# A two-layer hybrid trunk on one core: moving the second layer's set-up beside the first layer's gate and up products, and making the second layer's first product in passes

## The chip, the core and the metric

One core of a Trainium2 chip runs the whole program, in one launch. The metric is the device time from the first to the last instruction, with what the runtime adds around it, in microseconds (us). Each of the core's engines works through its own queue in order: TensorE (PE; its weight loads are PEld), VectorE (DVE), ScalarE (ACT), GpSimd (POOL) and SyncE (SP), which here only issues DMA transfers. Engines wait for each other and for transfers on semaphores.

## The reference

The program is a decoder trunk of two layers over 1024 tokens of width 1024, in float32. Each layer normalises its input, projects it once to 1440 columns, and gives these to three mixers: sliding-window attention, a state-space layer, and latent attention. The outputs are joined, projected back and added; then a normalised SwiGLU feed-forward part follows. What the change touches is the parameter arithmetic of the state-space layer and the order of the work around it:

```python
for l in range(DEPTH):
    h = rms_norm(x, ln1_g[l])
    proj = h @ w_in[l]
    q_a, k_a, v_a, u_b, c_q, c_kv, k_r = jnp.split(proj, IN_SPLITS, axis=-1)
    o_a = swa_attention(q_a, k_a, v_a, sinks[l], bias)
    o_b = s5_mixer(u_b, ssm_a_re[l], ssm_a_im[l], ssm_log_dt[l], ...)
    o_c = mla_attention(c_q, c_kv, k_r, positions, ...)
    x = x + jnp.concatenate([o_a, o_b, o_c], axis=-1) @ w_out[l]
    h = rms_norm(x, ln2_g[l])
    x = x + (jax.nn.silu(h @ w_gate[l]) * (h @ w_up[l])) @ w_down[l]
return rms_norm(x, final_g)

# in s5_mixer, per layer, from the parameters alone:
lam = lax.complex(a_re, a_im); dt = jnp.exp(log_dt)
a_bar = jnp.exp(lam * dt[:, None])                    # 16 groups x 64 states
b_bar = ((a_bar - 1.0) / lam)[..., None] * bmat
```

## The kernel before, in words

**Precision.** A float32 operand is split into a high part (a rounded copy, made by ScalarE) and a low part (the rest, made by VectorE or GpSimd). A product takes three matmuls: high by high, high by low, low by high (`mm3s`, `product`).

**Set-up.** `setup` runs once at the start, before the first layer. It loads x and transposes it, and then, at a lower priority, calls `setup_ssm` for both layers at once: the parameters of two layers lie side by side in 16 columns, 8 for each layer, and the angles and magnitudes of the powers of `a_bar` are made on VectorE in tiles of 128x640 (`ph`) and 128x256 (`e1`), with two sines on ScalarE. A loop over q (two for each layer) then writes one row of parameters each, `sp`, to the DRAM tensor `spd`. `ssm_tables(l, f)` (f is 0 or 1) reads such a row back as `par`, and makes from it the tables of one half of a layer's state-space part: complex products on VectorE (`cmul`, L966) and, for the last one, on GpSimd; transposes (L998, L1022) and small matmuls (L1036, L1037) on TensorE in the one bank `s5`; copies on ScalarE; and writes to the DRAM tensors `tabd` and `lagd`. The first layer's two calls stand in `setup`, followed by the rotary set-up (`setup_rope`). The second layer's two calls stand in the first layer's feed-forward part, after pair 2 and after pair 6 of its gate and up products.

**Feed-forward.** Gate and up, and down, are Strassen-like: an operand is cut in 2x2 blocks, and seven products replace eight. In `ffn`, `ffn_begin` makes the first products of pairs 0 to 3 ahead, and `ffn_pair` then makes the others, 14 products of 12 matmuls for a full pair, for eleven pairs; it yields after each product, before the product's bank is evacuated. Down runs over windows of (column block d, first pair, end pair), `WINDOWS`. At the first window of a d the residual x tiles 2d and 2d+1 are loaded from `xe`; the last window has d = 2 and is worked in the order `LAST` = (1, 6, 2, 7, 4, 5, 3). While gate and up run, the x tiles 2 to 7 are free; the tables use them as scratch (`Lent`).

**Change of layers.** The blocks of the feed-forward operand are tiles b{block}{slot}, with slots 3, 0, 1, 2, of which pool 1 holds 16. `normed` puts the next layer's normalised input, high and low part for each k and half h, into these tiles in the order of `BLOCKS[1]`, k in the order `KORD` = (0, 1, 6, 7, 2, 3, 4, 5). So a part can be written when the last down window has made its last product with the block. Then `in_u` and `project_plain` make the first product of the next layer: 24 matmuls for half 0, 24 for half 1, and behind them (`scales`) the sums of squares and the scale factors.

**Order of work.** The program is traced in the order of the Python code. A scheduler then simulates it, and puts each engine's queue in order by priority (place in the trace) and simulated readiness, so instructions can move ahead of their place. `issue_after(ins)` adds, for instructions traced in its block on the engine of `ins`, that they stand behind `ins` in that engine's queue; it adds no semaphore.

The lines that the prediction names: L231, L237, L240 and L243 are the helpers `tt`, `ts`, `stt` and `act`; L247 and L248 the high and low part of a split; L271 to L273 the three matmuls of `mm3s`; L534 the write to `spd`, L979 its read; L1001 the copies of C out of the bank; L1635 the feed-forward matmuls; L1892 the load of the residual.

## Time and profile before

| | us |
|---|---|
| median of three runs (2316.06 to 2323.11) | 2319.89 |
| profiled execution, its own time | 2313.62 |
| its span, first to last instruction | 2311.8 |
| TensorE matmuls in flight | 2172.3 |
| VectorE busy | 1637.8 |
| GpSimd busy | 1171.5 |
| ScalarE busy | 990.9 |

The profiled execution is one run of the program; it need not be one of the three that are timed. Busy times count an engine's instructions in flight. Matmuls overlap, so TensorE's row is not its share of peak, and its gaps are more telling than its sum. In the lists, an instruction's row gives start, time, engine, line, operation, output and input tiles (buffer numbers left out), shapes and count, and in brackets the idle time before it with what released it. [...]

### The profile page before, as it was taken

How to read it: one execution, taken by the hardware profiler on the slowest of the kernel's cores; microseconds unless marked ns; L12 is line 12 of the kernel's file. 1: busy time of each engine (PE TensorE's matmuls, PEld its weight loads, DVE VectorE, ACT ScalarE, POOL GpSimd, SP SyncE). 2: the span in 40 equal slices, each digit the busy share in tenths (PEclk: the TensorE clock that was granted, in tenths of full speed). 3: DMA queues.
4: the chain of work that ended last, by engine and by line, in shares of the span. 5: the costliest groups of instructions: out<-in, count | busy, mean ns of one | idle time of the engine just before them, and what ended most of it. 6: DMA issues, size and time to landing. Idle time of an engine off the chain costs nothing. (4 is left out here: it accounts for less than half of the span.)

```text
span 2311.8 us, 31478 instructions
## 1 busy us (share of the span) xinstructions
PE 2172.3 (94%) x10414; PEld 1775.8 (77%) x10414; DVE 1637.8 (71%) x2909; ACT 990.9 (43%) x1981; POOL 1171.5 (51%) x1038
## 2 busy tenths in 40 slices
PE   7699879999899999999979998799999999999998
PEld 6488768887778878788768886687877888877886
DVE  6677975559777677876855578655777756688767
ACT  5254665544232333444433456544522333254444
POOL 1263653134465555677743354530445555567765
PEclk9799999999999999999989999899999999999999
DMA  7622334543443353753333232535454332355422
GB/s 258 177 76 72 108 102 147 177 121 105 164 136 114 108 167 101 227 151 105 114 105 89 63 106 64 158 104 177 142 163 145 101 110 96 110 173 179 141 89 80
DMA packets 288300, 296.26 MB, mean 128 GB/s; under 512 B 43665, under 2 KB 213512, under 8 KB 288008
## 3 DMA queue, kind: packets, MB, share of 16 engines
q1 hardware_dynamic: 288136, 294.23, 41.6%
q8 instruction: 83, 1.36, 0.2%
q14 instruction: 81, 0.66, 0.1%
HBM read 204.63 MB, written 83.23 MB: 125 GB/s over the span
## 5 line engine op out<-in xcount | busy, mean ns | idle before, releaser
L1635 PE MATMUL f<-b,wt 128*128 128x512 f32 x3219 | 772.6, 395 | 20.0 <-ACT wt L247 5.1
L248 POOL TENSOR_TENSOR wt<-raw,wt 128x512 fp32r<-128x512 f32 (+3 forms) x332 | 497.9, 1506 | 534.7 <-ACT wt L247 398.1
L1635 PEld LDWEIGHTS f<-b,wt 128*128 128x128 f32 x3219 | 605.7, 189 | 164.3 <-ACT wt L247 7.1
L1635 PE MATMUL g<-b,wt 128*128 128x512 f32 x1965 | 477.9, 395 | 9.5 <-DVE gc L231 8.3
L1635 PEld LDWEIGHTS g<-b,wt 128*128 128x128 f32 x1965 | 370.0, 189 | 97.2 <-issue 10.5
L248 POOL TENSOR_TENSOR wt<-S,wt 128x512 fp32r<-128x512 f32 (+2 forms) x222 | 293.6, 1327 | 266.5 <-ACT wt L247 252.7
L247 ACT CAST wt<-raw 128x512 fp32r<-128x512 f32 (+3 forms) x356 | 229.3, 648 | 352.2 <-PE g L1635 93.9
L247 ACT CAST wt<-S 128x512 fp32r<-128x512 f32 (+2 forms) x222 | 126.2, 573 | 263.5 <-DVE S L1577 163.6
L271 PE MATMUL mm<-b,wt 128*128 128x512 f32 x320 | 131.4, 411 | 14.3 <-ACT b L243 13.5
L272 PE MATMUL mm<-b,wt 128*128 128x512 f32 x320 | 128.5, 402 | 0.9 <-DVE b L240 0.9
L273 PE MATMUL mm<-b,wt 128*128 128x512 f32 x320 | 128.2, 401 | 0.0
L248 DVE TENSOR_TENSOR tl<-pt,th 128x512 fp32r<-128x512 f32 (+2 forms) x176 | 96.4, 553 | 44.3 <-ACT th L247 41.9
L1577 DVE TENSOR_TENSOR S<-raw,raw 128x512 f32<-128x512 f32 (+2 forms) x74 | 65.5, 888 | 74.2 <-DMA raw<-in_w_gate 39.8
L247 ACT CAST th<-pt 128x512 fp32r<-128x512 f32 (+2 forms) x176 | 83.3, 477 | 78.9 <-PE pt L1308 41.4
L1290 POOL TENSOR_SCALAR pr<-pr,den 128x128 f32<-128x128 f32 (+3 forms) x64 | 49.1, 770 | 90.9 <-DVE den L1289 89.3
L1577 DVE TENSOR_TENSOR S<-raw,S 128x512 f32<-128x512 f32 (+2 forms) x74 | 81.9, 1110 | 13.2 <-POOL wt L248 13.1
L1635 PE MATMUL s<-b,wt 128*128 128x512 f32 x360 | 88.4, 393 | 2.2 <-DVE x L240 2.0
L902 POOL TENSOR_SCALAR pr<-pr,den 128x256 f32<-128x256 f32 (+1 forms) x128 | 70.6, 564 | 27.5 <-DVE den L900 22.1
L271 PEld LDWEIGHTS mm<-b,wt 128*128 128x128 f32 x320 | 62.0, 194 | 28.2 <-ACT b L243 14.6
L1635 PEld LDWEIGHTS s<-b,wt 128*128 128x128 f32 x360 | 67.8, 189 | 17.4 <-DVE x L240 2.5
L243 ACT ACTIVATE t<-B 128x512 f32<-128x512 f32 x44 | 27.8, 633 | 117.3 <-DVE B L231 116.6
L1281 PE MATMUL sc<-k,q 96*128 96x512 f32 (+7 forms) x288 | 73.0, 379 | 3.7 <-ACT pr L243 3.5
(472 smaller groups left out, 4124.0 us busy)
## 6 DMA issues: line engine op xcount, KB each, us to landing
raw<-in_w_gate SPq DMA_DIRECT2D x52, 512.0 KB, 4.0
raw<-in_w_up SPq DMA_DIRECT2D x52, 512.0 KB, 5.1
actd<-gc SPq DMA_DIRECT2D x102, 256.0 KB, 2.0
raw<-in_w_out SPq DMA_DIRECT2D x32, 512.0 KB, 3.9
B<-actd SPq DMA_DIRECT2D x62, 256.0 KB, 2.7
raw<-in_w_down SPq DMA_DIRECT2D x40, 384.0 KB, 3.3
x<-xe SPq DMA_DIRECT2D x48, 256.0 KB, 3.0
raw<-in_w_in SPq DMA_DIRECT2D x22, 512.0 KB, 5.3
```

Source lines behind the costliest of these rows:

```text
L243: self.A.activation(out=out, in_=a, func=func, **kw)
L247: self.A.copy(hi, src)
L248: (eng or self.V).tensor_tensor(out=lo, in0=src, in1=hi.bitcast(F32), op=ALU.subtract)
L271: self.T.matmul(ps, wh, xh, start=(i == 0), stop=False)
L272: self.T.matmul(ps, wh, xl, start=False, stop=False)
L273: self.T.matmul(ps, wl, xh, start=False, stop=(i == n - 1))
L902: self.G.tensor_scalar(out=pr[:, j, lo_k:256], in0=pr[:, j, lo_k:256], scalar1=den[:, j:j + 1], scalar2=0.0, op0=ALU.mult, op1=ALU.add)
L1281: self.T.matmul(o, q[a][rows, qs], k[kh][c][rows, 0:w], start=(x == 0), stop=(x == 2 and not last))
L1290: self.G.tensor_scalar(out=pr[:, 0:nk], in0=pr[:, 0:nk], scalar1=den[:, 0:1], scalar2=0.0, op0=ALU.mult, op1=ALU.add)
L1577: tt = lambda o, x, y, op: (self.G if b in self.gpre else self.V).tensor_tensor(out=o, in0=x, in1=y, op=op)
L1635: mm = lambda w, x, i: self.T.matmul(p, w, x, start=(i == 0 and not onto), stop=(i == 3 * n - 1), skip_group_check=onto)
```

## The change

1. `setup` calls `setup_ssm` for layer 0 alone, with 8 columns in place of 16. The 8 columns of layer 1's three parameters are kept in a small tile.
2. In the first layer's `ffn`, layer 1's `setup_ssm` and both calls of `ssm_tables` are recorded: their engine calls go to a list, not to the engines. After each product of pairs 4 to 10 three entries of the list are issued, on TensorE behind the last matmul and on VectorE behind the last `tt` or `stt`; what is left over is issued after the last pair. The set-up's tiles come from the same x tiles as the tables' (`Shelf`), and the row of parameters is one tile for each q.
3. The order of `BLOCKS[1]` is other: slot 3 of the five blocks first, as before, but then all slots of block 6, of 7, of 4, of 5, and of 3.
4. In the second layer `project_plain` makes its first product in passes over both halves: high weights by high input, low weights by high input, then high weights by low input, in turns of eight matmuls.
5. In `normed` for the second layer, the low parts of the last four k are placed on VectorE behind the last recorded `tt` or `stt`. `gained` itself is no longer recorded in `last_v`.

```diff
-BLOCKS = [[(b, k) for k in SLOTS for b in bs] for bs in ((1, 2), (6, 7, 4, 5, 3))]
+BLOCKS = [[(b, k) for k in SLOTS for b in (1, 2)], [(b, SLOTS[0]) for b in (6, 7, 4, 5, 3)]]
+BLOCKS[1] += [(b, k) for b in (6, 7, 4, 5, 3) for k in SLOTS[1:]]
 BLOCKS[1:] = BLOCKS[1][:16], BLOCKS[1][16:]
...
+class Recorder:
+    def __init__(self, engine, log):
+        self.engine, self.log = engine, log
+    def __getattr__(self, name):
+        return lambda *a, **k: self.log.append((getattr(self.engine, name), a, k))
...
-        self.V.tensor_tensor(out=out, in0=a, in1=b, op=op)
+        self.last_v = self.V.tensor_tensor(out=out, in0=a, in1=b, op=op) or self.last_v
...
         with self.tc.high_priority(offset=-LATE):
-            self.setup_ssm(st, cols, logdt, n16)
+            a_re, a_im = (cols[:, spans[x]:spans[x] + n16] for x in ("a_re", "a_im"))
+            self.ssm_in = [(a_re, a_im, logdt)]
+            for i in range(1, L):
+                keep = cp.tile([128, 3, 8], F32, f"ssm_in{i}")
+                for j, x in enumerate(self.ssm_in[0]):
+                    self.V.tensor_copy(keep[:, j], x[:, 8 * i:8 * i + 8])
+                self.ssm_in.append([keep[:, j] for j in range(3)])
+            self.setup_ssm(st, 0)
             self.setup_bias(st, ps)
...
-    def setup_ssm(self, st, cols, logdt, n):
-        are = cols[:, self.spans["a_re"]:self.spans["a_re"] + n]
-        aim = cols[:, self.spans["a_im"]:self.spans["a_im"] + n]
+    def setup_ssm(self, st, l):
+        n = 8
+        are, aim, logdt = (x[:, 0:n] for x in self.ssm_in[l])
...
-        sp = st.tile([128, 2 * self.depth, NSP], F32, "sp")
-        for q in range(2 * self.depth):
+        for q in range(2):
+            par = st.tile([128, NSP], F32, f"sp{q}")
...
-            self.dma(out=self.spd[q], in_=sp[:, q, :])
+            self.dma(out=self.spd[2 * l + q], in_=par)
...
     def project_plain(self, l, c0, evac, w=None, then=None, tag=("mm", 2)):
         wh, wl = w or self.in_weights(l, c0)
         done = []
+        if l and then is not None:
+            done = [self.mps.tile([128, 512], F32, *tag) for _ in range(2)]
+            passes = [(wh, 0, k) for k in KORD] + [(wl, 0, k) for k in KORD] + [(wh, 1, k) for k in KORD]
+            for a in range(0, 24, 8):
+                for h, p in enumerate(done):
+                    for i in range(a, a + 8):
+                        x, j, k = passes[i]
+                        self.T.matmul(p, x[:, k, :], self.h[h][k][j], start=(i == 0), stop=(i == 23))
+            then(2)
+            for h, p in enumerate(done):
+                evac(h, p)
+            return
...
-            self.gained(self.xT[k][h], self.spans["ln1"] + 8 * l + k, t[k])
+            order = self.tc.issue_after(self.last_v.ins) if l and n > 3 else contextlib.nullcontext()
+            with order:
+                self.gained(self.xT[k][h], self.spans["ln1"] + 8 * l + k, t[k])
...
+    def recorded(self, *parts):
+        for part in parts:
+            log = []
+            kept = self.V, self.A, self.T, self.G, self.dma
+            self.V, self.A, self.T, self.G = (Recorder(e, log) for e in kept[:4])
+            self.dma = lambda **k: log.append((kept[4], (), k))
+            part()
+            self.V, self.A, self.T, self.G, self.dma = kept
+            for f, a, k in log:
+                with self.tc.issue_after(self.last.ins), self.tc.issue_after(self.last_v.ins):
+                    f(*a, **k)
+                yield
...
         if more:
-            tabp = Lent([lambda i=i: self.x_tile(2 + i % 6, i // 6, False) for i in range(12)], ("bbr", "bbi", "cr", "ci", "dg"))
+            places = [lambda i=i: self.x_tile(2 + i % 6, i // 6, False) for i in range(12)]
+            tabp = Lent(places, ("bbr", "bbi", "cr", "ci", "dg"))
+            side = self.recorded(lambda: self.setup_ssm(Shelf(places), l + 1),
+                                 *(lambda f=f: self.ssm_tables(l + 1, f, tabp, ps, None) for f in range(2)))
         drain(ahead)
         for pair in range(FT // 2):
-            drain(self.ffn_pair(l, pair))
-            if more and pair in (2, 6):
-                with self.tc.issue_after(self.last.ins):
-                    self.ssm_tables(l + 1, pair // 4, tabp, ps, None)
+            for _ in self.ffn_pair(l, pair):
+                if more and pair > 3:
+                    next(side, None), next(side, None), next(side, None)
+        if more:
+            drain(side)
```

## Rows read from the trace of the kernel before

**Rows 1.** The page, part 1: busy us (share of span) x instructions.
```profile
PE 2172.3 (94%) x10414; PEld 1775.8 (77%) x10414; DVE 1637.8 (71%) x2909; ACT 990.9 (43%) x1981; POOL 1171.5 (51%) x1038
```

**Rows 2.** Windows at the start: length, busy PE, PEld, DVE, ACT, POOL, PEclk, DMA, GB/s.
```profile
65.00:84.40 19.40, 0.00 (x0) 0.00 (x0) 12.63 (x80) 2.30 (x3) 2.73 (x1) 0.58 0.61 154
84.40:92.00 7.60, 5.87 (x16) 3.81 (x17) 6.50 (x11) 2.40 (x5) 5.06 (x8) 0.51 0.58 172
```

**Rows 3.** Waits from 60 to 130 us: us in total, times, longest.
```profile
PE s L1022 <- DVE t L966: 19.6, 1, 19.6
...
DVE bbr L966 <- DMA par<-spd: 6.6, 1, 6.6
```

**Rows 4.** Timeline of VectorE at the start.
```profile
40.42 0.23 DVE L544 CAST rang<-pos 128x128 f32<-128x128 int32 x1 [2.22 <-DMA xd<-x]
...
67.74 0.20 DVE L510 COPY sp<-sn 128x96 f32<-128x96 f32 x1
...
74.07 0.47 DVE L231 TENSOR_TENSOR sp<-sp,q 128x4 f32<-128x4 f32 x4
```

**Rows 5.** Timeline of TensorE in the first layer's gate and up.
```profile
647.60 0.33 PE L998 MATMUL s<-ident,x 128*128 128x128 f32 x1 [4.72 <-DVE x L1001]
647.69 4.12 PE L1635 MATMUL g<-b,wt 128*128 128x512 f32 x10
```

**Rows 6.** Windows of 40 us in the first layer's gate and up.
```profile
740.00:780.00 40.00, 40.00 (x176) 32.73 (x175) 24.17 (x31) 12.56 (x21) 19.72 (x15) 1.00 0.32 101
780.00:820.00 40.00, 40.00 (x182) 32.20 (x181) 31.04 (x47) 12.69 (x23) 23.27 (x20) 1.00 0.37 117
```

**Rows 7.** Timeline of TensorE at the change of layers.
```profile
1186.98 0.76 PE L271 MATMUL mm<-b,wt 128*128 128x512 f32 x1 [12.27 <-ACT b L243]
```

**Rows 8.** Timeline of VectorE at the change of layers.
```profile
1175.84 2.83 DVE L240 SCALAR_TENSOR_TENSOR b<-x,gains,b 128x512 fp32r<-128x512 f32 x1
...
1186.16 0.68 DVE L240 SCALAR_TENSOR_TENSOR x<-f,x 128x512 f32<-128x512 f32 x1
```

**Rows 9.** Groups by line and shape, VectorE, 38 to 76 us: busy, mean ns | idle.
```profile
L231 DVE TENSOR_TENSOR ph<-ph,phr 128x640 f32<-128x640 f32 x2 | 1.6, 821 | 0.0
L237 DVE TENSOR_SCALAR phr<-ph 128x640 f32<-128x640 f32 x2 | 1.0, 485 | 0.0
...
L231 DVE TENSOR_TENSOR mag<-e1y,e1e 128x256 f32<-128x256 f32 x1 | 0.4, 421 | 0.0
...
L237 DVE TENSOR_SCALAR e1k<-e1k 128x256 f32<-128x256 f32 x2 | 0.6, 289 | 0.0
```

**Rows 10.** Timeline of the DMA queue of SyncE at the start.
```profile
75.67 0.32 SPq L564 DMA_DIRECT2D ropec<-rwide  x1
...
78.11 0.46 SPq L979 DMA_DIRECT2D par<-spd  x1
```

**Rows 11.** Timeline of TensorE over gate and up of both layers.
```profile
494.85 8.40 PE L1635 MATMUL f<-b,wt 128*128 128x512 f32 x35 [1.15 <-DVE b L1611]
...
947.46 7.00 PE L1635 MATMUL f<-b,wt 128*128 128x512 f32 x30
...
1628.99 8.39 PE L1635 MATMUL f<-b,wt 128*128 128x512 f32 x35 [1.15 <-DVE b L1611]
...
1788.17 5.71 PE L1635 MATMUL f<-b,wt 128*128 128x512 f32 x24 [1.73 <-DVE gc L231]
```

**Rows 12.** The chain that ended last, at the end of layer 1's gate and up.
```profile
2070.08 2.81 PE f L1635 x12
```

**Rows 13.** Groups of ScalarE over the whole span: busy, mean ns | idle before.
```profile
L243 ACT ACT_TABLE_LOAD x3 | 3.8, 1283 | 4.3 <-DVE nm L894 3.5 <-PEq L1992 0.7
```

**Rows 14.** Window of the instructions of L966: length, DVE, POOL, PEclk, DMA, GB/s.
```profile
820.00:840.00 20.00, 2.67 (x4) 5.46 (x6) 1.00 0.41 120
```

**Rows 15.** Timeline of the DMA queue of SyncE after the turn to down.
```profile
965.62 0.42 SPq L1892 DMA_DIRECT2D x<-xe  x1
```

**Rows 16.** Window of the second layer's first product, columns as in rows 2.
```profile
1186.98:1199.80 12.82, 12.82 (x48) 10.43 (x49) 1.98 (x2) 1.20 (x2) 1.60 (x3) 0.85 0.48 140
```

More of the change, by code (lines that the diff above doesn't have):

```diff
@@ L1 @@
+import contextlib
 import itertools
@@ L148, in tile, with __init__ @@
         return t[0:shape[0], o:o + n].rearrange(f"p ({names}) -> p {names}", **dims)
+class Shelf:
+    def __init__(self, makers):
+        self.makers, self.at, self.t, self.end = list(makers), {}, None, 512
+    def tile(self, shape, dt, tag, bufs=1):
+        n = int(np.prod(shape[1:]))
+        if tag not in self.at:
+            if self.end + n > 512:
+                self.t, self.end = self.makers.pop(0)(), 0
+            self.at[tag] = self.t, self.end
+            self.end += n
+        t, o = self.at[tag]
+        t = t[0:shape[0], o:o + n]
+        if dt != F32:
+            t = t.bitcast(dt)
+        names = " ".join(f"a{i}" for i in range(len(shape) - 1))
+        return t.rearrange(f"p ({names}) -> p {names}", **{f"a{i}": x for i, x in enumerate(shape[1:])})
+class Recorder:
[3 more added lines that the diff above has]
+        return lambda *a, **k: self.log.append((getattr(self.engine, name), a, k))
 class Weave:
@@ L524, in setup_ssm @@
             self.V.reciprocal(out=den, in_=den)
-            wr, wi = sp[:, q, 324:328], sp[:, q, 328:332]
+            wr, wi = par[:, 324:328], par[:, 328:332]
             self.tt(wr, nr, lr, ALU.mult)
@@ L1831, in keep_blocks, with ffn @@
             put(4, a[0, 0])
-    def ffn(self, l, tp, side, other):
+    def recorded(self, *parts):
[10 more added lines that the diff above has]
+                yield
+    def ffn(self, l, tp, where, other):
         P = self.pools
@@ L1849, in ffn @@
         tp.close()
-        self.sqp = P.open("squares", side)
+        self.sqp = P.open("squares", where)
         self.sq = [[None, None] for _ in range(2)]
         for i in (1, 2):
-            self.blkp[i] = self.blocks(i, side)
+            self.blkp[i] = self.blocks(i, where)
         kept = [lambda: self.sqp.tile([128, HALF], F32, "sq", 3)] * 3 + [lambda h=h: self.sqp.tile([128, HALF], F32, f"acc{h}", 1) for h in range(2)]
```

9 lines of the change are left out of this document (5 added, 4 removed).

## The prediction

> **What bounds the kernel now.** I read the page first: over the span TensorE has matmuls in flight 94% of the time, VectorE is busy 71% [rows 1]. So time can only come out of the places where TensorE has nothing. I looked for those with windows over the slices in which the page's PE digit is low, then with the lists of waits, then with the timeline of the engine that TensorE waited for. The change touches three such places.
>
> (a) Start: TensorE is empty from 65.0 to 84.4 us [rows 2]. The next instruction in its queue is a transpose of the first layer's tables, which waits 19.6 us for VectorE [rows 3]. VectorE works from 40.4 to 74.5 us, in one piece, on the set-up of the state-space layer for both layers, mixed with the rotary set-up and four evacuations [rows 4]; then it waits 6.6 us for `par`, which goes through DRAM [rows 3].
>
> (b) The first layer's gate and up phase: one wait stands out, 4.7 us of TensorE for a copy out of the bank of the tables (L998 on L1001) [rows 5]. In the seven 40 us windows from 660 to 940 us TensorE has no gap, and VectorE is busy 60 to 80%; two of the seven are shown [rows 6].
>
> (c) Change of layers: after the last down product TensorE is empty for 12.3 us, until 1186.98 [rows 7]. VectorE has no gap there, in 14 instructions of which the first and the last are shown [rows 8].
>
> **The change part by part.**
>
> *Half of the set-up leaves the start.* Except in the loop over q, VectorE's instructions become narrower, not fewer. A tensor_tensor takes 0.82 us with 640 columns and 0.42 with 256, so 1.04 ns a column; a tensor_scalar 0.485 and 0.289, so 0.51 ns [rows 9]. On the 128x640 tiles six of the first kind and three of the second lose 320 columns: 2.0 + 0.5 us. The second exponential and `xm` lose 128 columns in eleven and seven: 1.5 + 0.5 us. Instructions with 16 columns stay as long as they are. The loop over q runs twice in place of four times: its four passes fill 67.74 to 74.54 us but for two wide instructions of `phr` and `cs` between them (some 1.1 us by the rates above), so 5.7 us, half of it 2.85 [rows 4]. Added are three small copies into `ssm_in1`, about 0.25 us. Net 7.1 us of a queue without gaps, so all of it is path as far as 74.5. Behind it, the sync queue has two writes of `spd` fewer ahead of the read of `par`, but the read also stands behind a rotary write, which waits for its own data [rows 10]. The rotary set-up moves less, about 4 us, since the loop over q comes after it. So the read can move by 6 to 7.1 us; I take **6.8 us**. The ends: 4 us, if the rotary writes decide alone, and 9 us, if most of the 2.4 us between rotary write and read comes on top. [...] The same queue orders stay in front of what follows, so I keep the whole gain to the end; were it given back at the next wait, it would be 0.
>
> [...]
>
> *The second layer's set-up and tables go into pairs 4 to 10, three recorded instructions per product.* I count 113 instructions of set-up and 105 for each of two calls of `ssm_tables`, 323 in all; there is room for 7 x 14 x 3 = 294, so 29 come after the last product. What goes: the tables no longer sit in pair 2. Layer 1 has the same phase without any tables and shows their price: it takes from 1628.99 to 2072.9 us, 443.9 us, against 458.1 from 494.85 to 952.9 in layer 0 (24 matmuls of its last group belong to this phase) [rows 11, 12]. Of these 14.2 us some 9 are the tables' own matmuls (64 small ones at 0.11 us, 20 transposes at about 0.1) and stay. The stall of 4.7 us goes, with the ten matmuls behind it that ran at half the clock (4.0 us rather than 2.3): 6.4 us [rows 5]. But layer 1 has a boundary wait of 1.7 us at pair 3 [rows 11], from which the stall saves layer 0 today, and that comes back. Gain **4.7 us**; bounds 6.4 and, if one such stall stays among the new ones, 0. The work added to VectorE is some 13 us of set-up in 105 us, on top of 60 to 78% [rows 6]: it fits. The evacuation of the next product stands behind at most three of these instructions, mostly small ones, with several banks of slack in front of TensorE. The added DMAs go into a sync queue that has loads ahead by a product or more; nothing.
>
> ScalarE must load the sines' table in the middle of this phase. The trace has three table loads in all, 1.28 us each [rows 13], so two more are 2.6 us on an engine that is busy 30% there [rows 6]. It makes every high part of the weights; with five buffers of weights in front I cost it at nothing, and at 2.6 us if that cover is gone. [...]
>
> *29 instructions at the turn to the down phase.* Among them are six operations on GpSimd (5.5 us in the second call now [rows 14]) and two writes of tables, and their tiles are those into which the residual of the first down window is loaded. One of these four loads is issued as late as 965.6 us even now [rows 15], a dozen us into the down phase, so there is some tolerance. I take a **loss of 1.5 us**; ends 0 and 5 (all of GpSimd's work in the open).
>
> *The change of layers.* From 1175.84 to the end of the last residual add at 1186.84 are 11.0 us [rows 8]. In them VectorE does seven adds, 4.3 us at 0.6, and seven low parts `b`, 6.7 us. With the new order the low parts of the last four k stand behind the last add, and those of the first four have their blocks earlier (slot 3 and block 6 are the first that the last window lets go). One of the seven takes 2.83 us beside GpSimd's split of a weight, rather than 0.7 like the others; that stretch falls on an add or two instead, so I count 5.5 of the 6.7 us: last add near 1181.3, last high part some 0.7 us later. The passes need only high parts for the first 32 matmuls, so it doesn't matter whether the bank or the high part releases the first of them. The block of 48 matmuls took 12.8 us from 1186.98, at a mean granted clock of 0.85 [rows 16]; that stays. Eight low parts behind the add take 5.3 us, to 1187; the third pass begins near 1190. So the block ends at about 1194.3 rather than 1199.8: **5.5 us**. Ends: 2 us if VectorE's low parts stay in front, 8 if the first matmuls run ahead of the last add.
>
> Sum: 6.8 + 4.7 - 1.5 + 5.5 = 15.5 us. Against the profiled execution, 2313.62 us (2311.8 of span and 1.8 around it), that is 2298.1. This execution was 6.3 us below the median of the three runs, 2319.89; the forecast is for a median, so **2304.4 us**.
>
> **Rivals.**
>
> *Stalls per product (slower).* Place: the twenty points in pairs 6 to 10 at which a transpose or small matmul of the tables stands in TensorE's in-order queue behind a product and waits for VectorE or ScalarE. Price: the one stall there is cost 6.4 with the clock [rows 5]. Against: ten such points of the second call lie in windows without a gap [rows 6]; for: the first call had the stall. With 15.5 us gained elsewhere, two or three stalls (12.8 to 19.2) cancel it, and from four on the kernel is slower: 25.6 - 15.5 = 10 us, **2330 us**.
>
> *Transfers bound the start.* The rotary writes and the DRAM round trip decide there, 3 us, and the turn to the down phase takes its 5: 15.5 - 3.8 - 3.5 = 8, **2312 us**. For it: the DMA engines are 61% busy in the gap [rows 2].
>
> *The passes bring nothing*: the bank, or the order on VectorE, holds the first matmul as long as now, and only 2 us come from the blocks; then 12 us, **2308 us**.
>
> *It does not do what it says*: the scheduler orders by simulated times and puts the recorded work so that the gains are eaten at other boundaries: **2317 us**.
>
> **How the numbers follow.** Forecast 0.53, start bound by transfers 0.12, no gain from the passes 0.11, nothing in sum 0.14, stalls 0.10. About 0.3% (7 us) is what a measurement of this kernel can tell from no change; 2312.9 is that border. The first three cases are faster (the second barely), so faster 0.76, same 0.14, slower 0.10. Range 2293 (most of the upper ends) to 2318 (nothing in sum).
>
> **What would show it.** Right: TensorE's gap at the start ends near 78 us; no wait of several us on L1001 in the first layer's gate and up phase; a gap of about 6 us at the change of layers. Wrong: waits of TensorE on `s` in pairs 4 to 10, a load of `x` from `xe` long after the first down window, a gap that ends after 82 us at the start, or a first product that still begins 12 us after the last down product.

## The result, and the profile of the changed kernel

The changed kernel takes 2334.22 us (median of four runs, 2328.2 to 2336.77) beside 2319.92 us for the kernel before on the same chip: a ratio of 1.0059, 95% interval 1.0032 to 1.0085. It is 0.6% slower, and the interval lies above 1; the forecast was 2304.4 us, with a range from 2293 to 2318. The execution that was profiled took 2328.2 us, with a span of 2326.0 us, 14.2 us longer than the span before. The page shows the same share of TensorE and 17.4 us more of VectorE, in 75 more instructions [rows 1]:

```profile
PE 2180.6 (94%) x10414; PEld 1777.5 (76%) x10414; DVE 1655.2 (71%) x2984; ACT 988.9 (43%) x1985; POOL 1175.2 (51%) x1038
```

The sum hides six stages that moved in different directions. I cut both spans at rows of TensorE's timeline: the first ffn matmul, the last gate and up product (the start of the wait for `us` at the turn), the last down product, the end of the block of 48 matmuls, the first ffn matmul of the second layer.

| stage (us) | before | after | difference | forecast |
|---|---|---|---|---|
| start and mixers, first layer | 493.3 | 489.6 | -3.7 | -6.8 |
| its gate and up | 465.7 | 471.5 | +5.8 | -4.7 |
| its down phase, with the turn | 215.7 | 230.4 | +14.7 | +1.5 |
| change of layers | 25.3 | 19.8 | -5.5 | -5.5 |
| mixers of the second layer | 427.5 | 433.2 | +5.7 | 0 |
| its ffn and the end | 684.4 | 681.5 | -2.9 | 0 |

Each stage is read from one execution of each kernel. How far one such reading carries, the kernels of this document show: in the start, five of them (the kernel before, e1_passes, e6_tables, e9_copies and e14_fills) have the same instructions in the same order on every engine, and take 493.3 to 502.9 us. Gate and up and the down phase vary less where nothing was changed in them: gate and up 463.6 to 466.2 us in three kernels, down 215.4 to 216.6 us in six. So a few us in the start are no finding from one execution.

**Start.** In VectorE's timeline the first layer's set-up now ends at 61.5 us, 13 us earlier than before [rows 4], and the wait for `par` behind it is as long as it was [rows 3]:

```profile
61.07 0.48 DVE L265 TENSOR_TENSOR sp<-sp,q 128x4 f32<-128x4 f32 x4
68.45 0.23 DVE L1019 TENSOR_TENSOR bbr<-par,t 128x64 f32<-128x64 f32 x1 [6.91 <-DMA par<-spd]
```

TensorE's gap, which ended at 84.4 us before, ends at 71.8 us, with another wait of 2.65 us close behind. But what follows in its queue is now all of the first `ssm_tables` call, and the first dense product comes at 89.8 us, 1.7 us later than the 88.1 us of before:

```profile
71.76 0.66 PE L1075 MATMUL s<-ident,t 128*128 128x128 f32 x2 [8.26 <-DVE t L1019]
75.06 0.69 PE L1075 MATMUL s<-ident,t 128*128 128x128 f32 x2 [2.65 <-DVE t L1019]
...
89.77 0.79 PE L305 MATMUL mm<-b,wt 128*128 128x512 f32 x1
```

The sync queue shows why the dense product could not go first: the loads of its weights stand behind all sixteen writes of `ud`, the two of `spd` and the read of `par`. Before, they were issued at 56 us, behind eight of the writes of `ud`.

```profile
55.45 8.00 SPq L746 DMA_DIRECT2D ud<-u  x14
63.55 0.86 SPq L575 DMA_DIRECT2D spd<-sp  x2
64.47 0.94 SPq L746 DMA_DIRECT2D ud<-u  x2
66.04 0.34 SPq L1032 DMA_DIRECT2D par<-spd  x1
66.48 0.40 SPq L297 DMA_DIRECT2D raw<-in_w_in  x1
66.93 1.52 SPq L604 DMA_DIRECT2D rwide<-rbropec  x3
68.55 0.40 SPq L297 DMA_DIRECT2D raw<-in_w_in  x1
```

**Gate and up.** The wait of 4.72 us on the bank of the tables [rows 5] is gone. In its place TensorE's timeline has the boundary wait that was expected (651.61) and three waits of 1.5 to 2.7 us in which a recorded transpose or small matmul stands in its queue while VectorE is not done with the operand; L1899 is the line from which the recorded instructions are issued:

```profile
651.61 5.73 PE L1690 MATMUL g<-b,wt 128*128 128x512 f32 x24 [2.35 <-DVE gc L265]
789.88 0.33 PE L1899 MATMUL s<-ident,x 128*128 128x128 f32 x1 [2.69 <-DVE x L1899]
918.23 0.38 PE L1899 MATMUL s<-x,x 64*16 64x128 f32 x2 [2.08 <-DVE x L1899]
949.76 0.41 PE L1899 MATMUL s<-ident,x 128*128 128x128 f32 x2 [1.52 <-DVE x L1899]
```

**Turn to the down phase.** The largest loss. TensorE waits for a weight, for left-over instructions, and at 991.77 for a residual add (L274), which empties the bank that its next product needs. Then two windows of that stretch, after and before: TensorE is busy for less of them, and the granted clock (PEclk, the third figure from the end; 1.00 is full speed) is 0.83 and 0.91 in place of 0.91 and 1.00.

```profile
970.66 0.74 PE L1690 MATMUL f<-b,wt 128*128 128x512 f32 x2 [3.52 <-ACT wt L281]
972.75 0.58 PE L1899 MATMUL s<-x,x 64*16 64x128 f32 x2 [1.35 <-DVE x L1899]
...
991.77 8.54 PE L1690 MATMUL g<-b,wt 128*128 128x512 f32 x29 [3.46 <-DVE x L274]
```
```profile
960.00:980.00 20.00, 12.09 (x42) 7.62 (x43) 17.79 (x25) 8.89 (x19) 16.85 (x14) 0.83 0.89 311
980.00:1000.00 20.00, 16.54 (x69) 12.74 (x68) 9.77 (x16) 5.44 (x11) 8.36 (x9) 0.91 0.61 195
```
```profile
960.00:980.00 20.00, 18.19 (x71) 13.95 (x72) 18.14 (x25) 9.44 (x19) 16.18 (x14) 0.91 0.85 274
980.00:1000.00 20.00, 20.00 (x88) 16.31 (x87) 14.84 (x17) 9.00 (x16) 13.95 (x12) 1.00 0.30 89
```

Loads of the residual are late: they go out as late as 982 us and after, behind the last writes of the tables (`tabd`) that sat in the same tiles. In the kernel before, the late one of the four went out at 965.62 [rows 15].

```profile
978.53 0.32 SPq L1965 DMA_DIRECT2D x<-xe  x1
979.83 0.38 SPq L1626 DMA_DIRECT2D raw<-in_w_down  x1
980.38 0.39 SPq L1973 DMA_DIRECT2D B<-actd  x1
981.97 0.32 SPq L1899 DMA_DIRECT2D tabd<-x  x1
982.34 2.72 SPq L1965 DMA_DIRECT2D x<-xe  x4
```

But the wait at 991.77 is not a wait for such a load alone. In VectorE's queue the add stands behind work on the next weights (L1632), which waits 3.0 us for GpSimd's low part of a weight; no wait for a transfer shows in front of the add itself:

```profile
986.28 0.69 DVE L274 SCALAR_TENSOR_TENSOR x<-f,x 128x512 f32<-128x512 f32 x1 [0.30 <-DMA x<-xe]
989.97 0.56 DVE L1632 TENSOR_TENSOR S<-S,raw 128x384 f32<-128x384 f32 x1 [3.00 <-POOL wt L282]
990.56 0.56 DVE L1632 TENSOR_TENSOR raw<-raw 128x384 f32<-128x384 f32 x1
991.03 1.41 DVE L274 SCALAR_TENSOR_TENSOR x<-g,x 128x512 f32<-128x512 f32 x2
```

**Change of layers.** The passes do what they were to do: seven matmuls right behind the last down product, a gap of 5.8 us in place of 12.3 [rows 7], and the rest almost without a break:

```profile
1191.79 1.85 PE L714 MATMUL mm<-b,wt 128*128 128x512 f32 x7 [0.24 <-DVE x L274]
1199.42 0.80 PE L714 MATMUL mm<-b,wt 128*128 128x512 f32 x1 [5.78 <-ACT b L277]
1200.61 10.69 PE L714 MATMUL mm<-b,wt 128*128 128x512 f32 x40 [0.39 <-DVE x L274]
```

### The profile page after: what moved, and what is told of

The parts are those of the page before. It is cut to its first block, busy times and chain, and to the rows that moved or that the text cites. A ratio compares the mean times of both kernels' runs of the same rounds, so it can differ in the third digit from the quotient of the medians.

```text
span 2326.0 us, 31542 instructions
## 1 busy us (share of the span) xinstructions
PE 2180.6 (94%) x10414; PEld 1777.5 (76%) x10414; DVE 1655.2 (71%) x2984; ACT 988.9 (43%) x1985; POOL 1175.2 (51%) x1038
## 5 line engine op out<-in xcount | busy, mean ns | idle before, releaser
L282 POOL TENSOR_TENSOR wt<-S,wt 128x512 fp32r<-128x512 f32 (+2 forms) x222 | 300.4, 1358 | 260.5 <-ACT wt L281 256.5
L305 PE MATMUL mm<-b,wt 128*128 128x512 f32 x304 | 125.4, 413 | 0.1
L306 PE MATMUL mm<-b,wt 128*128 128x512 f32 x304 | 121.5, 400 | 0.2 <-DVE b L700 0.2
L1632 DVE TENSOR_TENSOR S<-raw,raw 128x512 f32<-128x512 f32 (+2 forms) x74 | 68.7, 931 | 74.3 <-DMA raw<-in_w_gate 37.5
L307 PE MATMUL mm<-b,wt 128*128 128x512 f32 x304 | 121.5, 400 | 0.0
L1632 DVE TENSOR_TENSOR S<-raw,S 128x512 f32<-128x512 f32 (+2 forms) x74 | 75.7, 1026 | 10.5 <-POOL wt L282 10.4
L1632 DVE TENSOR_TENSOR S<-S,raw 128x512 f32<-128x512 f32 (+2 forms) x74 | 68.2, 921 | 10.9 <-POOL wt L282 10.9
```

The lines of the kernel that those rows point to most:

```text
L282: (eng or self.V).tensor_tensor(out=lo, in0=src, in1=hi.bitcast(F32), op=ALU.subtract)
L305: self.T.matmul(ps, wh, xh, start=(i == 0), stop=False)
L306: self.T.matmul(ps, wh, xl, start=False, stop=False)
L307: self.T.matmul(ps, wl, xh, start=False, stop=(i == n - 1))
L1632: tt = lambda o, x, y, op: (self.G if b in self.gpre else self.V).tensor_tensor(out=o, in0=x, in1=y, op=op)
```

## The experiments

Each kernel was timed with the kernel before on the same chip (6 to 12 runs of it, 23 to 35 of the kernel before). Stages are cut as in the table above, from one profiled execution each.

| run | median us | ratio to before, 95% | start | gate, up | down | change | mixers 2 |
|---|---|---|---|---|---|---|---|
| e1_passes | 2315.12 | 0.9987 (0.9973 to 1.0002) | 498.1 | 463.6 | 215.7 | 22.1 | 425.5 |
| e2_early | 2326.39 | 1.0034 (1.0020 to 1.0048) | 488.6 | 482.8 | 216.4 | 21.3 | 427.6 |
| e3_hold | 2323.36 | 1.0020 (1.0006 to 1.0034) | 489.2 | 477.4 | 216.1 | 21.6 | 429.2 |
| e4_place | 2328.61 | 1.0048 (1.0030 to 1.0067) | 493.9 | 474.6 | 226.1 | 21.7 | 430.1 |
| e5_four | 2326.63 | 1.0038 (1.0022 to 1.0055) | 491.0 | 479.8 | 215.8 | 21.4 | 431.1 |
| e6_tables | 2316.22 | 0.9980 (0.9966 to 0.9993) | 502.9 | 464.5 | 215.7 | 22.1 | 425.2 |
| e7_ud | 2335.40 | 1.0074 (1.0058 to 1.0090) | 492.7 | 471.5 | 231.8 | 20.5 | 432.4 |
| e8_all | 2326.68 | 1.0029 (1.0013 to 1.0044) | 490.9 | 478.5 | 217.0 | 21.8 | 433.6 |
| e9_copies | 2319.91 | 0.9994 (0.9979 to 1.0008) | 501.2 | 467.4 | 216.6 | 21.6 | 428.5 |
| e10_gap | 2329.10 | 1.0030 (1.0013 to 1.0047) | 505.4 | 466.2 | 215.4 | 22.6 | 432.2 |
| e11_gaptables | 2328.04 | 1.0027 (1.0015 to 1.0038) | 509.2 | 465.1 | 217.4 | 22.7 | 433.0 |
| e12_gpsimd | 2324.18 | 1.0015 (0.9998 to 1.0031) | 496.3 | 476.1 | 219.6 | 22.4 | 422.7 |
| e13_tail | 2324.04 | 1.0019 (1.0003 to 1.0035) | 494.9 | 472.5 | 219.0 | 21.7 | 430.1 |
| e14_fills | 2315.53 | 0.9986 (0.9973 to 0.9999) | 500.5 | 463.3 | 215.4 | 22.5 | 431.8 |

### The passes alone

The kernel before, with the change's BLOCKS, project_plain and normed; its core:

```diff
+        if l and then is not None:
...
+            order = self.tc.issue_after(self.last_v.ins) if l and n > 3 else contextlib.nullcontext()
```

> The kernel before with the change of layers alone changed (passes, new order of the blocks, low parts behind the last add); set-up and tables as before. Theory A (the parts add up, and the passes are worth what the two traces show between the last down product and the end of the block of 48 matmuls, 25.1 us before and 19.6 us after): the same 19.6 us here, last down product and gate and up phase where they were, and the second layer's mixers, from that block to the first ffn product, still 429.2 us; total 2319.9 - 5.5 = 2314.4 us. Rival B (the passes only move the time: both banks of the first product close together, and the second layer's mixers lose what the block gained; in the trace after they take 434.9 us): 19.6 us, but mixers of about 435 us, total 2320 us.

The block ends 22.1 us behind the last down product, 3.2 us earlier than in the kernel before, and the mixers don't give it back (425.5 against 427.5). So theory A in kind, with 3 us in place of 5.5; the median is 3.4 us below the kernel before on that chip (2318.53), and the interval just reaches 1. The second layer's mixers of the changed kernel, 433.2 us, are not the passes' doing.

### The turn: what is left over, where its scratch lies, and when it is issued

e2_early, e4_place (two tables to a tile) and e13_tail, each against the changed kernel:

```diff
-                if more and pair > 3:
+                if more and pair > 0:
```
```diff
-            places = [lambda i=i: self.x_tile(2 + i % 6, i // 6, False) for i in range(12)]
-            tabp = Lent(places, ("bbr", "bbi", "cr", "ci", "dg"))
+            places = [lambda i=i: self.x_tile(4 + i % 4, i // 4, False) for i in range(8)]
+            tabp = Packed(places)
```
```diff
-                    next(side, None), next(side, None), next(side, None)
+                    for _ in range(3 if pair < 10 else 6):
+                        next(side, None)
```

> The changed kernel with the recorded work beginning in pair 1 in place of pair 4, three instructions per product as before, so that it ends in pair 8 and nothing is left for the down phase. Theory A (the turn to the down phase lost some 14 us because the 29 instructions left over ran there): the stretch from the last gate and up products to the last down product of the first layer is again as in the kernel before, 13 to 15 us shorter than after; the stalls of TensorE on recorded instructions in the gate and up phase stay (6.7 us idle after); total 2334 - 14 = 2320 us. Rival B (the turn was lost to the new order of transfers or of the weights' splits, whatever of the tables runs there): 2334 us.

> The changed kernel, same instructions at the same products, 29 of them still left over for the down phase; only their scratch is packed into the tiles of the residual for k 4 to 7, so that those of k 2 and 3, which the first down window adds to, are free early. Theory A (the turn is lost because the residual of the first window is loaded into tiles that the left-over instructions still use, so its adds and with them the banks come late): loads of x from xe for the first window at about 950 to 966 us as before, no wait of several us on the residual add near 990 us, total 2334 - 8 = 2326 us. Rival B (it is lost to the left-over instructions themselves on ScalarE, GpSimd, VectorE and TensorE): 2332 to 2334 us.

> The changed kernel with one difference: in the last pair six recorded instructions per product are issued in place of three, so that the 29 left over are issued before the down phase; everything up to pair 9 is as there. Theory A (the turn's loss of some 15 us is the price of these 29 alone, 4 of it by the tiles that they share with the first window's residual, as the run with other scratch showed, and the rest by their place among the down products): turn 216 to 218 us in place of 230, gate and up phase 471 to 474 us as after, total 2334 - 13 = 2321 us. Rival B (they cost as much in pair 10, where VectorE has 75% of its time taken): gate and up phase 480 us as in the run with four per product, total 2328 us.

The turn follows what is left over: 230.4 us with it, 216.4 when the work starts early, and 219.0 in the last run, in which the same 29 instructions are issued a few products earlier and nothing else is changed; gate and up stays at 472.5 there. The median falls from 2334.2 to 2324.0. Theory A of the last run holds. The other scratch gave back 4.3 of the 14.7 us (226.1), where its theory A named 8: the shared tiles are a part, and the greater part is these instructions among the down products themselves (its rival B). How that part divides between TensorE's, VectorE's and GpSimd's queues was not tested. The run with other scratch still waits 3.5 us on a residual add, now near 1008 us, and e13_tail still waits 2.6 us for a weight near 975.

What the early start gains at the turn it loses in gate and up (482.8): both runs that begin in pair 1 have this wait at the boundary of two pairs, where the changed kernel has 2.35 us:

```profile
657.56 8.59 PE L1690 MATMUL g<-b,wt 128*128 128x512 f32 x24 [8.95 <-DVE gc L265]
```

### Gate and up: holding TensorE's instructions back, and how many per product

In recorded(), and in ffn() for e3_hold (pair > 0) and e5_four (pair > 3, range(4)):

```diff
+                if f.__self__ is kept[2] and was is not kept[2]:
+                    yield True
...
-                    next(side, None), next(side, None), next(side, None)
+                    for _ in range(3):
+                        if next(side, None):
+                            break
```

> As the run that begins in pair 1, and a recorded TensorE instruction that follows one of another engine is held back until the next product, so that it stands a product of about 2.9 us or more behind its producer. Theory A (the stalls come from transposes and small matmuls queued directly behind a product while their operands are still in VectorE's queue): the idle time of TensorE on recorded instructions falls from some 6.7 us to under 2 us and the dips of the clock behind them go; 5 to 8 us below the run that begins in pair 1, 2313 us. Rival B (VectorE is behind by more than a product there, so the wait is only moved): no difference, 2320 us.

> The changed kernel with the recorded work from pair 4 as there, but four instructions per product, and a recorded TensorE instruction that follows one of another engine held back to the next product; all of it is issued before the last product. Theory A (three prices that add up: work left over at the turn costs 14 us, operands just queued cost TensorE 4 to 6 us, and set-up ahead of pair 4 costs another 9 us, the wait of 8.9 us of TensorE on gc near 657 us that both runs beginning in pair 1 have and the changed kernel has with 2.4): turn as in the kernel before (216 us against 230 after), gate and up phase of 465 to 468 us (471.5 after, 477 in the run with held instructions from pair 1), the wait near 652 us at 2 to 3 us; total 2334 - 14 - 5 = 2315 us. Rival B (VectorE has no room anywhere in this phase, wherever the work begins): gate and up phase of 477 us again, 2323 us.

Holding back works: the waits on recorded instructions behind the boundary are 1.1 and 1.2 us where the run without it has 1.2, 2.9 and 1.2, and the stage is 5.4 us shorter. But the boundary's 8.8 us stays, so the total is 10 us above what theory A gave. With four per product from pair 4 the boundary wait is 2.7 us, as theory A says, and yet the stage takes 479.8 us: waits on `gc` (1.8 us near 732) and on recorded operands (2.9, 2.7, 3.3 us) come elsewhere. Rival B of that run holds: wherever set-up and tables are put, this phase grows by 6 to 17 us over the 465.7 us of before. That turned the question from where the instructions stand to what they cost.

### Is it the tables or the set-up?

On top of e1_passes, with the set-up left at the start and TensorE's instructions held back:

```diff
+            tables = self.recorded(*(lambda f=f: self.ssm_tables(l + 1, f, tabp, ps, None) for f in range(2)))
...
-            if more and pair in (2, 6):
-                with self.tc.issue_after(self.last.ins):
-                    self.ssm_tables(l + 1, pair // 4, tabp, ps, None)
```

> The kernel before with the passes (as the run of the passes alone), and of the rest only this: the second layer's two calls of ssm_tables (210 instructions) recorded and issued three per product from pair 4, with TensorE's held back to the next product; the set-up for both layers stays at the start. Theory A (recording the tables brings what was forecast, the stall of 4.7 us and the slow clock behind it go and a boundary wait of some 2 us comes; it is the set-up of 113 more instructions that has no room): gate and up phase 463.6 - 4 = 459 to 460 us, total 2315 - 4 = 2311 us. Rival B (issuing per product costs as much as the blocks did): 463 to 466 us, 2315 us or more.

The 210 recorded instructions of the tables cost the stage nothing (464.5 against 463.6) and bring nothing either: the wait of 3.9 us on the first table of the other run is gone, and waits of 0.7 to 0.9 us at a boundary and on two recorded instructions stand in its place, with the waits at the earlier boundaries a little longer: TensorE is idle for 11.5 us of the stage, and for 12.1 in e1_passes. Rival B in size. So the 8 us that runs with the recorded set-up have over runs without it (472.5 on average in after, e4_place, e7_ud and e13_tail, 464.6 in before, e1_passes and e6_tables) go with the set-up's 113 instructions. (This run also holds TensorE's instructions back, which those four don't; but the runs that hold back with the set-up in it, e3, e5 and e8, take 477.4 to 479.8 us, so holding back alone doesn't give the 8 us.) VectorE's time points the same way. In the stage, recorded instructions take 68.2 us of VectorE in the changed kernel (176 of them) and 38.2 us here (76), so the set-up takes at least 30 us, where the forecast had 13. It is nearer 35: eight of the tables' instructions, 5.2 us, ran behind the stage in the changed kernel. The groups by shape in the changed kernel show how; columns as in [rows 9]:

```profile
L1899 DVE TENSOR_TENSOR x<-x 128x8 f32<-128x8 f32 x17 | 7.3, 445 | 0.3
L1899 DVE TENSOR_SCALAR x<-x 128x8 f32<-128x8 f32 x16 | 6.0, 386 | 0.2
...
L1899 DVE SCALAR_TENSOR_TENSOR x<-x 128x128 f32<-128x128 f32 x2 | 2.6, 1292 | 0.1
```

A tensor_tensor or tensor_scalar of 8 columns, which takes 0.16 us at the start, takes 0.45 or 0.39 us here on average. In the timeline, the long ones lie beside GpSimd's splits of the weights:

```profile
675.12 1.27 DVE L1899 TENSOR_SCALAR x<-ssm_in 128x8 f32<-128x8 f32 x1
676.42 2.49 DVE L1899 TENSOR_SCALAR x<-x 128x8 f32<-128x8 f32 x2
678.95 0.37 DVE L1899 SCALAR_TENSOR_TENSOR x<-x 128x8 f32<-128x8 f32 x2
```
```profile
672.89 3.47 POOL L282 TENSOR_TENSOR wt<-S,wt 128x512 fp32r<-128x512 f32 x2
676.32 2.56 POOL L282 TENSOR_TENSOR wt<-raw,wt 128x512 fp32r<-128x512 f32 x2
```

### The price of a small instruction by itself

On top of e1_passes, 113 in all, three per product from pair 4; the copies, and the fills in their place:

```diff
+                            self.V.tensor_copy(self.idle, self.gains[:, 0:8])
```
```diff
-                            self.V.tensor_copy(self.idle, self.gains[:, 0:8])
+                            self.V.memset(self.idle, 0.0)
```

> The kernel of the run with the passes alone (set-up at the start, tables in their two blocks) with 113 copies of 8 columns on VectorE added, whose result nobody reads, three per product from pair 4. Theory A (it is the number of small VectorE instructions that has no room in this phase: an instruction that takes 0.16 us alone takes up to 1.3 us beside GpSimd's splits, and the set-up's 108 took some 30 us there, 68.2 less the tables' 38.2, in place of the 13 us of the forecast): the copies take about 30 us of VectorE, 0.27 us each, and the gate and up phase becomes 6 to 9 us longer than 463.6; total 2315 + 7 = 2322 us. Rival B (what costs is something else in the set-up: its wide instructions, its table load on ScalarE, its chain of dependences): copies at about 0.1 us each, 11 us, gate and up phase within 2 us of 463.6, 2315 us.

> The run with 113 small copies, with 113 fills of the same 8 columns (memset, no input) in place of the copies. In that run every copy of more than 0.5 us that stands alone in the trace overlaps a GpSimd instruction (6 of 6, 1.1 us on average), those that don't take 0.16 us. [...] Rival B (VectorE is held up beside GpSimd whatever it does, or 113 more instructions in its queue cost 4 us by their number): fills of over 1 us as well, or 467 us again, 2320 us.

The source line's own list (count, ns as min/median/max, first and last start) of the copies and of the fills:

```profile
L1892 DVE COPY idle<-gains x113: 156/172/1283, 690.3 to 791.7; 128x8 f32<-128x8 f32 x113
```
```profile
L1892 DVE MEMSET idle<- x113: 65/65/65, 689.0 to 785.9; 128x8 f32 x113
```

A copy takes 0.17 us in the median and 1.28 us at most, 45.6 us in all, and a fill never more than 0.065, 7.3 us in all. Of the 113 copies, the 77 that overlap no GpSimd instruction take 0.17 us each; the 36 that do take 0.90 us on average, 30 of them more than 0.5. Of the fills 85 overlap one, and take 0.065 us like the others. So rival B of the fills fails: no fill gets longer beside GpSimd, and the phase is not 467 us again. That copies get longer there is what the forecast missed. The longest, 1.28 us, is about one of GpSimd's splits (1.27 to 1.50 us between 700 and 716 us of e9_copies); what makes a copy longer there was not shown.

What these longer copies are worth is less firm. Gate and up is 467.4 us with the copies, 463.3 with the fills and 463.6 to 466.2 with nothing added, and the medians, 0.9994 and 0.9986 of the kernel before, don't tell the two runs apart. Theory A of the copies holds in kind (45.6 us of VectorE, with 30 expected), but the stage is 1 to 4 us longer and not 6 to 9. Only the run with the copies has these two waits of TensorE on the tables' transposes; e1_passes and e14_fills have none there:

```profile
807.75 0.33 PE L1014 MATMUL s<-ident,x 128*128 128x128 f32 x1 [1.36 <-DVE x L1017]
813.90 0.41 PE L1038 MATMUL s<-ident,x 128*128 128x128 f32 x2 [1.02 <-DVE x L1017]
```

Nor is VectorE's time all that the set-up costs: in this stage VectorE is busy for 384.2 us with the copies and for 375.2 in the changed kernel, whose stage is 4.1 us longer. The rest of the set-up's 8 us I put down to the chain behind it, whose operands come late for TensorE (the waits on L1899 above); that part was argued from the trace and not taken away by itself.

The last one is e5_four with the recorded set-up's copies, tensor_tensor and tensor_scalar on GpSimd:

```diff
+            if not n:
+                self.V = Recorder(kept[3], log, kept[0])
```

> The run with four instructions per product from pair 4 and TensorE's held back, with the recorded set-up's copies, tensor_tensor and tensor_scalar on GpSimd in place of VectorE (its few other instructions stay). Theory A (VectorE's queue is what has no room): gate and up phase back to 466 to 470 us from 479.8, total 2327 - 11 = 2316 us. Rival B (GpSimd holds up the low parts of the weights, or VectorE beside it, as much): 2327 us or more.

Between the two: gate and up 476.1 us, 3.7 us better than with VectorE, not the 10 us of theory A. VectorE is busy for 354.6 us of the stage here, close to the 350.7 of the kernel before, and the stage is still 10.4 us longer than there: TensorE waits 7.1 us on recorded instructions and 3.3 us on `gc` near 705. So the added VectorE time is not enough to explain the stage; whether the rest is GpSimd's time (284.5 us in place of 253.4) or the chain was not separated.

### The start: loads out of the way, and the second set-up in the wait

e7_ud against the changed kernel (e8_all is this on top of e5_four), and e10_gap, with the tables in their two blocks (e11_gaptables: recorded as in e6_tables):

```diff
-            self.dma(out=dst[g], in_=u2[16 * g:16 * g + 16])
+            (self.dma if l else self.A.dma_start)(out=dst[g], in_=u2[16 * g:16 * g + 16])
```
```diff
             self.setup_rope(st)
+            self.setup_ssm(st, 1)
```

> The changed kernel with one difference at the start: the sixteen writes of ud of the first layer are issued from ScalarE's queue in place of the sync queue, so that the loads of the next weights don't stand behind them. Theory A (VectorE's set-up ends 13 us earlier, but the first dense product behind the gap doesn't, since its weights were loaded only at 66.5 and 68.6 us, behind these writes, and so the tables' 40 small instructions were queued in front of it): weights are loaded near 55 us, TensorE's gap ends near 71 us as after and the first dense product begins near 75 us rather than 89.8; first ffn product 8 us earlier than after, total 2334 - 8 = 2326 us. Rival B (the stretch up to 250 us is bound by VectorE and the tables' own chain, not by when dense products begin): first ffn product within 2 us of after, 2334 us.

> Both together: four per product from pair 4 with TensorE's held back, and the writes of ud from ScalarE's queue. If the prices add up (theory A of both runs): 2334 - 14 - 5 - 8 = 2307 us, below the kernel before by 12 us. If the start's gain is given back and VectorE has no room (rivals B): 2323 us.

> The changed kernel's passes and its set-up split by layers, but the second layer's set-up stays at the start, issued behind the first layer's tables, so that it fills the 6.9 us in which VectorE waits for par; the tables are in their two blocks as before. Theory A (beside an idle GpSimd 113 small instructions cost about 0.1 us each, and half of them fall into a wait): first ffn product about 490 us as after, 8 us earlier than in the run with the passes alone (498.1), the other stages as there; total 2315 - 7 = 2308 us. Rival B (the other half of the set-up holds up the evacuations of the first dense products, and the pool that the mixers reuse comes free later): 2315 to 2320 us.

> As the run with the second set-up in the wait for par, with the tables recorded, three per product from pair 4, TensorE's held back to the next product (as in the run with recorded tables alone). Since recording the tables changed the gate and up phase by 1 us (464.5 against 463.6), theory: within 3 us of the run with the second set-up in the wait, 2306 to 2311 us if that run is at 2308. Rival (the tables' block at pair 2 and the set-up at the start are not independent, since the recorded tables come after all of the start): 2315 us.

With the writes of `ud` out of the sync queue the weights are loaded at 56.8 and 59.5 us and the first dense product starts at 78.84 us, 9.2 us earlier than in the kernel before:

```profile
75.20 0.66 PE L1075 MATMUL s<-ident,t 128*128 128x128 f32 x2 [11.59 <-DVE t L1019]
...
78.84 0.80 PE L305 MATMUL mm<-b,wt 128*128 128x512 f32 x1 [0.76 <-DVE c L1151]
```

The lead holds up to 243 us (a wait for `k` of 2.47 us that the kernel before has at 251.90 stands at 242.89), and at the first ffn matmul it is 0.6 us. That execution of the kernel before is the fastest of the five with its start; against their mean, 499.2 us, the two kernels with the writes moved (492.7 and 490.9) are 7.4 us ahead, and the seven with the changed kernel's start (491.9) are as far ahead without it. So the queue was the reason for the late dense product (A), but rival B holds for the end: the earlier dense product gains nothing at the first ffn matmul. What takes the lead up behind 243 us was not followed. e8_all adds nothing to e5_four, and its theory A, 2307 us, fails.

The other way round, the second layer's set-up at the start behind the first one's tables makes the first ffn matmul come at 505.4 us, against 498.1 in the run with the passes alone, and with recorded tables 509.2: rival B in kind, though the medians, 2329 and 2328 us, lie well above its 2320; in both, the second layer's mixers are some 7 us longer as well (432.2 and 433.0 against 425.5). There was room in VectorE's wait for `par`, but the instructions spill over into the first layer's tables (TensorE's first dense product is at 94.28 us there). Taking the set-up away from the start is worth something only if it goes away from there altogether.

## Why the prediction was wrong

**The step that failed first is the term of the turn**, the "loss of 1.5 us" with ends 0 and 5. It measured 14.7 us by the stage, and 11.4 of it come back when the 29 instructions are issued before the down phase (230.4 to 219.0). I counted GpSimd's 5.5 us and the writes, and took one late load [rows 15] as tolerance. I didn't count that sixteen small matmuls of the tables stand in TensorE's in-order queue between down products, that residual tiles can't be loaded until the tables in them are written (982 us; other scratch gave back 4.3 us), that the adds then come late in VectorE's queue and hold the banks, or the clock: 0.83 and 0.91 in two windows. Idle time of TensorE in the stage is 14.5 us against 5.2; the rest, about 5 us, I put down to the clock (an estimate of 3.4 us: 0.08 and 0.09 of 20 us in the two windows) and to the left-over matmuls.

**The second is the term of gate and up**, "Gain 4.7 us", with its reason "The work added to VectorE is some 13 us of set-up in 105 us". The stage lost 5.8 us. The set-up's work measured 30 to 35 us; the duration was taken from the start, where GpSimd is busy for 8.0 of 36.5 us, and used where it is busy half of the time (253.4 of 465.7 us). That explains a part: 113 copies that took about as much of VectorE's time cost the stage 1 to 4 us, and with most of the set-up off VectorE the stage was still 10 us longer. The rest lies, as far as is known, in TensorE's waits on recorded operands, and its cause stays open. Two more table loads on ScalarE cost nothing, as forecast: they stand at 711 and 719 us, 1.28 us each, where TensorE has no wait. The stall did go and the boundary wait did come back (2.35 us for the 1.7 expected), but the stall's removal by itself, tested with the tables alone, gave nothing (464.5 against 463.6): the other waits took up the slack.

**The start** was right in size, by luck, and wrong in its chain. The forecast's -6.8 is -3.7 between the two profiled executions; over the seven kernels with this start the first ffn matmul stands at 491.9 us on average, over the five with the old one (before, e1_passes, e6_tables, e9_copies, e14_fills) at 499.2, so -7.3. But VectorE was ready 13 us earlier, not 7. Of the three splits on GpSimd that stood beside the set-up before, the last (64.82 to 67.73 us) now comes behind it; beside it a tensor_scalar of 128 columns had taken 1.78 us that takes 0.22 now, and the queue's idle time fell from 2.5 to 0.5 us. The gap ended at 71.8 and not 78, and these 12.6 us were not kept: the first dense product came 1.7 us later than before, since its weights' loads stood behind `ud`, and a later stretch sets the end, for in e7_ud, without that delay, the first ffn matmul comes no earlier. "The same queue orders stay in front of what follows" was untrue.

**The change of layers** was right, with -5.5 us and a gap of 5.8 us for the 6 named. But the size is in part luck: alone (e1_passes) it is worth 3 us, and the 19.8 us of the changed kernel are the shortest of the fifteen kernels with the passes, which take 21.7 on average. Why it is shorter there was not shown.

**The rival** "stalls per product" named the place and came close to the time (2330 us), but not by its price, so the time is luck: four waits on recorded instructions, 6.7 us in all, not four at 6.4, and the turn made up the rest.

**Not settled:** the second layer's mixers, where nothing was changed, took 422.7 to 433.6 us over these kernels, 427.5 before and 433.2 after. VectorE's and ScalarE's instructions stand there in one order in the changed kernel, e7, e8, e10 and e11, which take 432.2 to 433.6 us, and in another in nine of the kernels with the passes, which take 422.7 to 431.8, 428.0 on average. So some 5 us go with the order, and most of the 5.7 us of the result with them; which instructions make it was not followed. With one and the same order, single executions still differ by 9 us (422.7 in e12_gpsimd, 431.8 in e14_fills), with a granted clock of 0.969 and 0.968 over the whole execution.

A version better than both is e6_tables, the passes with recorded tables and the set-up at the start: 0.9980 (0.9966 to 0.9993) of the kernel before. The passes alone, 0.9987, can't be told from it.

## What to carry to other kernels

Take the duration of a moved instruction from the stage into which it goes, not from the one that it leaves: copies of 8 columns took 0.90 us on average beside a GpSimd instruction here and 0.17 us away from one (e9_copies). That price is not yet the loss: ask also which engine waits for the results. When work is spread over a phase in fixed portions, work out where the last portion lands; what spills over the border sits in front of the next phase's first loads, and a portion doubled in the last steps costs far less. A lead that is won at the start is worth only what the next stretch that waits for other engines lets through.

## What the runs showed of the hardware

VectorE copies of 8 columns took 0.17 us alone and up to 1.28 us while GpSimd ran an instruction (e9_copies); a fill of the same size took 0.065 us every time, GpSimd or not (e14_fills).

In the run with `ud` on ScalarE's queue TensorE was busy for more of the window from 340 to 360 us than in the kernel before (17.76 against 16.00 us), with fewer matmuls in it (61 against 71), and the granted clock was 0.60 against 0.83 there; it had been busy 15.09 of the 20 us in front of it. The first two rows are that run's, the third is the kernel before's. The two windows hold different work, since the run is ahead, so they don't show that its lead went there.

```profile
320.00:340.00 20.00, 15.09 (x83) 12.42 (x84) 14.22 (x38) 14.68 (x36) 17.88 (x18) 0.80 0.54 154
340.00:360.00 20.00, 17.76 (x61) 13.07 (x60) 10.98 (x18) 10.71 (x20) 4.00 (x4) 0.60 0.80 226
```
```profile
340.00:360.00 20.00, 16.00 (x71) 12.75 (x72) 11.68 (x29) 10.91 (x24) 3.67 (x4) 0.83 0.89 281
```
